# Two transformer blocks on one core: the seams between stages, in what order they issue loads, weight splits and projections

## The chip, the cores and the metric
The kernel runs on one core of a Trainium2 chip. The metric is the device time of one execution in microseconds (us); lower is better. A core has TensorE (PE, matrix products into PSUM banks), VectorE (DVE), ScalarE (ACT), GpSimd (POOL) and SyncE (SP, which only issues transfers). Each engine works off its own list of instructions in order and waits on semaphores of the others.

## The reference, cut to what matters
Two blocks follow each other on 256 tokens of width 1024. The first block has two layers of attention and a mixture of 32 experts, over 256 latent and 256 context tokens; its last layer returns the latent tokens alone. The second block has two layers ("last layers" below) of a mixer with three branches and a gated feed-forward net, each closed by a layer norm.

```python
# first block, end of each layer
h_lat = layer_norm(ALPHA * h_lat + mods[:, :, 5] * y_lat, ln_g[i, 1], ln_b[i, 1])   # y: the experts' output, mods[5]: gate
# second block
for l in range(2):
    mix = hybrid_mixer(x, w_in[l], ...)          # projections a_q, a_k, a_v, ..., attention, conv, MoBA, gates
    x = layer_norm_2(ALPHA_2 * x + mix, ln1_g[l], ln1_b[l])
    ffn = (silu(x @ w_gate) * (x @ w_up)) @ w_down
    x = layer_norm_2(ALPHA_2 * x + ffn, ln2_g[l], ln2_b[l])
```

## The kernel before
Tokens lie in tiles of 128: two latent tiles (`hlat`) and, in the first block, two context tiles (`hctx`). Every dense product is made in three: the activations and the weights are each split into a high part (rounded to fp32r) and a low part (the rest), and `mm3` (lines 178 to 180) adds high x high, high x low, low x high. `project` does this for one weight of 512 (or 256) columns: for each token tile 8 x 3 = 24 products into one bank, then an evacuation.

`dense` (line 166 and 167) fetches one weight in pieces of 1 MB: SP issues the load into a ring of six raw tiles (`wraw`; line 143), ACT copies each half of a piece to its high part (L166), DVE (or POOL where told) subtracts to get the low part (L167). The parts go to tiles `whl` of a pool with six buffers; a weight of 512 columns takes four, the key/value weight of the mixer (`proj{l}` number 13, 256 columns) two. `prefetch` issues loads ahead of their `dense`.

`to_hilo` makes the input of a projection: PE transposes a token tile to two banks (L225), one bank is scaled and shifted by DVE (L235) and one by ACT (L233) with the norm's gain and bias as columns, ACT copies the high part (L238), DVE subtracts for the low part (L239). `normalize` is two DVE statistics (L338), an aggregate (L331), a scale (L211), a power on POOL (L213), and one operation over the tile, on DVE (L341) or on ACT (L345 after L344).

Four places lie around the change.
1. After the first expert stage, `combine` loads for each of four tiles two expert outputs (`y`, L1211) and, once for each pair of tiles, a gate row broadcast to all partitions (L1213), all on SP, with weight loads between (`ahead`). The function that it returns combines one tile (L1219 to L1222) and normalizes it. `layer1_attention` calls it for four tiles; the first weight, `cd_in` 0, is split from the second tile on, and its instructions are put behind the norm of that tile by `issue_after`.
2. After the second expert stage the same `combine` runs for two tiles. `block2(0)` opens its pools (`hi2`, `xT2`, `ev2`), `take` does both tiles, and `mixer2` then projects: weight 13 for both tiles, weight 0 (queries `aq`) for both tiles, weight 1 (`cq`), and so on; attention work fills in between.
3. At the end of layer 0's `ffn2` the four results are added to `hlat` (L1573) and normalized; `block2(1)` opens new pools over the memory of the old ones.
4. At the end of layer 1's `ffn2` each tile is normalized, multiplied by a gain row and shifted by a bias row (L349, L350) and stored from ACT's queue (L1577).

The order of each engine's list is not the order of the calls: a planner (`schedule_with_timeline_sim`) simulates the program, and at each point gives an engine the earliest-called instruction that is ready by its own costs. Loads, splits, transposes and products of neighbouring stages are therefore mixed. A tile pool's buffer is given out again when all users of the old content are done; a new pool over old memory waits in the same way. Expert branches are units that nothing crosses.

## Time and profile before

| | us |
|---|---|
| median of 3 runs (lowest to highest) | 2293.49 (2291.16 to 2294.03) |
| profiled execution | 2294.27 |
| span of its profile | 2292.1 |
| PE busy | 1927.0 (84%) |
| DVE busy | 1005.3 (44%) |
| ACT busy | 732.4 (32%) |
| POOL busy | 263.3 (11%) |

The span is the time from the first to the last instruction of the profiled execution. PE's busy time is that of its products, which overlap a little; its granted clock over the span is 0.919 of full speed on average (full speed or half, the half in pauses and shortly after them). The expert stages, where loads bind, end near 780 and 1302 us; the second block runs from there to the end, with its layers meeting at 1800 us.

### The profile page before, as it was taken

How to read it: one execution, taken by the hardware profiler on the slowest of the kernel's cores; microseconds unless marked ns; L12 is line 12 of the kernel's file. 1: busy time of each engine (PE TensorE's matmuls, PEld its weight loads, DVE VectorE, ACT ScalarE, POOL GpSimd, SP SyncE). 2: the span in 40 equal slices, each digit the busy share in tenths (PEclk: the TensorE clock that was granted, in tenths of full speed). 3: DMA queues.
4: the chain of work that ended last, by engine and by line, in shares of the span. 5: the costliest groups of instructions: out<-in, count | busy, mean ns of one | idle time of the engine just before them, and what ended most of it. 6: DMA issues, size and time to landing. Idle time of an engine off the chain costs nothing. (4 is left out here: it accounts for less than half of the span.)

```text
span 2292.1 us, 27169 instructions
## 1 busy us (share of the span) xinstructions
PE 1927.0 (84%) x10066; PEld 1342.1 (59%) x10066; DVE 1005.3 (44%) x1968; ACT 732.4 (32%) x1304; POOL 263.3 (11%) x205
## 2 busy tenths in 40 slices
PE   6999797777886489976876469998999799998997
PEld 2656476333443267753333157787788677776886
DVE  3346665410000174561000057656554467566554
ACT  2233432100111254410101055544444355434442
POOL 0002401101101152120111002000100020002000
PEclk9999698799998799977998779999999999998999
DMA  9973204454779651157589654354455444354550
GB/s 395 364 298 128 103 28 173 179 196 186 306 287 364 254 228 63 42 203 282 220 341 407 244 218 165 111 183 161 157 184 181 149 158 139 135 176 159 184 179 29
DMA packets 74302, 456.05 MB, mean 199 GB/s; under 512 B 12696, under 2 KB 13244, under 8 KB 23648
## 3 DMA queue, kind: packets, MB, share of 16 engines
q1 hardware_dynamic: 61632, 430.99, 50.0%
q0 software_dynamic: 8816, 14.79, 1.8%
q10 hardware_dynamic: 3632, 7.37, 0.9%
q8 instruction: 132, 2.16, 0.4%
q14 instruction: 90, 0.74, 0.1%
HBM read 452.77 MB, written 13.30 MB: 203 GB/s over the span
## 5 line engine op out<-in xcount | busy, mean ns | idle before, releaser
L167 DVE TENSOR_TENSOR whl<-w,whl 128x1024 fp32r<-128x1024 f32 x312 | 395.5, 1282 | 230.3 <-ACT whl L166 220.2
L166 ACT ACTIVATE whl<-w 128x1024 fp32r<-128x1024 f32 x332 | 344.4, 1057 | 259.9 <-PE bankA L180 208.1
L178 PE MATMUL bankA<-whl,x2h 128*128 128x512 f32 (+1 forms) x864 | 344.2, 399 | 9.7 <-ACT x2h L238 7.3
L180 PE MATMUL bankA<-whl,x2l 128*128 128x512 f32 (+1 forms) x864 | 343.8, 398 | 6.2 <-DVE x2l L239 6.2
L179 PE MATMUL bankA<-whl,x2h 128*128 128x512 f32 (+1 forms) x864 | 340.8, 395 | 0.0
L1073 PE MATMUL bankA<-w,xt 128*128 128x512 f32 x320 | 156.7, 652 | 46.7 <-issue 37.1
L178 PEld LDWEIGHTS bankA<-whl,x2h 128*128 128x128 f32 x864 | 167.7, 194 | 43.7 <-ACT x2h L238 8.3
L180 PEld LDWEIGHTS bankA<-whl,x2l 128*128 128x128 f32 x864 | 166.4, 193 | 40.7 <-DVE x2l L239 7.4
L179 PEld LDWEIGHTS bankA<-whl,x2h 128*128 128x128 f32 x864 | 167.2, 194 | 34.6 <-issue 2.0
L1073 PEld LDWEIGHTS bankA<-w,xt 128*128 128x128 f32 x320 | 66.4, 211 | 134.6 <-issue 133.7
L178 PE MATMUL bankA<-whl,xh 128*128 128x512 f32 (+1 forms) x336 | 132.7, 395 | 5.4 <-ACT xh L238 5.4
L179 PE MATMUL bankA<-whl,xh 128*128 128x512 f32 (+1 forms) x336 | 129.2, 384 | 5.1 <-DVE whl L167 5.1
L180 PE MATMUL bankA<-whl,xl 128*128 128x512 f32 (+1 forms) x336 | 128.2, 385 | 0.1
L1020 PE MATMUL bankA<-w,xt 128*32 128x256 f32 x1216 | 86.4, 428 | 48.8 <-issue 25.4
L414 ACT ACTIVATE p<-bankS,sm 128x256 f32<-128x256 f32 (+2 forms) x160 | 85.7, 537 | 117.7 <-DVE sm L405 60.3
L213 POOL TENSOR_TENSOR sm<-sm,mhalf 128x1 f32<-128x1 f32 (+3 forms) x32 | 32.1, 1004 | 691.4 <-DVE sm L211 679.6
L1020 PEld LDWEIGHTS bankA<-w,xt 128*32 128x32 f32 x1216 | 46.9, 122 | 88.6 <-issue 55.1
L1077 DVE TENSOR_TENSOR s<-s,bankA 128x512 f32<-128x512 f32 x10 | 6.9, 688 | 209.3 <-PE bankA L1073 196.6
L1002 POOL DMA_INDIRECT ybuf<-ys,stab x34 | 34.8, 1023 | 514.8 <-ACT xt L999 126.1
L178 PEld LDWEIGHTS bankA<-whl,xh 128*128 128x128 f32 x336 | 64.5, 192 | 33.0 <-ACT xh L238 7.4
L1024 DVE TENSOR_TENSOR s<-s,bankA 64x256 f32<-64x256 f32 x19 | 8.0, 423 | 169.6 <-ACT s L1023 169.6
L1088 PE MATMUL bankA<-w,ht 128*128 128x512 f32 x160 | 71.3, 599 | 7.8 <-DVE ht L1082 7.8
(462 smaller groups left out, 2921.6 us busy)
## 6 DMA issues: line engine op xcount, KB each, us to landing
w<-in_wmoe SPq DMA_DIRECT2D x174, 1024.0 KB, 15.0
w<-in_wd SPq DMA_DIRECT2D x166, 1024.0 KB, 5.5
w<-in_wmod SPq DMA_DIRECT2D x48, 1024.0 KB, 8.5
y<-ybuf SPq DMA_DIRECT2D x12, 512.0 KB, 10.1
w<-in_rows SPq DMA_DIRECT2D x5, 1024.0 KB, 5.4
w<-mrow SPq DMA_DIRECT2D x7, 512.0 KB, 11.0
fbuf<-w SPq DMA_DIRECT2D x4, 512.0 KB, 2.8
nb<-in_nabias POOLq DMA_DIRECT2D x16, 128.0 KB, 2.4
```

The lines of the kernel that those rows point to most:

```text
L166: nc.scalar.activation(h, s, AF.Copy)
L167: self.low = (eng or nc.vector).tensor_tensor(lo, s, h, ALU.subtract).ins
L178: mm(out, lhsT=xh, rhs=wh, start=start, stop=False)
L179: mm(out, lhsT=xh, rhs=wl, start=False, stop=False)
L180: mm(out, lhsT=xl, rhs=wh, start=False, stop=stop)
L213: self.power = self.nc.gpsimd.tensor_tensor(r, t, self.mhalf[:, :n], ALU.pow).ins
L414: nc.scalar.activation(p[:, :n], s[i][:, :n], AF.Exp, bias=nm[:, i:i + 1], accum_out=ss[:, i:i + 1])
L1002: nc.gpsimd.indirect_dma_start(out=ybuf.rearrange("r (m d) -> (r m) d", m=1 << parts), out_offset=bass.IndirectOffsetOnAxis(ap=stabs[parts ...
L1020: nc.tensor.matmul(acc[r:r + 32], lhsT=xT[:, k, 0:32], rhs=wslice(W, m, k, 256 * f, 256), start=k == 0, stop=k == KT - 1)
L1024: nc.vector.tensor_tensor(s, s, acc[64:128], ALU.mult)
L1073: nc.tensor.matmul(acc[m], lhsT=xT[:, k], rhs=wslice(W, m, k), start=k == 0, stop=k == KT - 1)
L1088: nc.tensor.matmul(yb[m], lhsT=hT[:, k], rhs=w2slice(W, k, m * 512, 512), start=k == 0, stop=k == 3)
```

## The change
- `combine` issues the gate rows first, on ACT's queue, and no longer on SP behind the first `y`; the lists `ahead` are laid out anew: after the first expert stage both pieces of `cd_in` 0 stand behind the first tile's `y`, after the second all first weights stand behind both tiles' `y`.
- `cd_in` 0 is split from the first tile on, behind the norm of that tile.
- `block2` of both layers shares its pools (`second_stage`). At the end of layer 0's feed-forward net, ahead of its norm, layer 1's first two weights (13 and 0) are called (`self.ready`), into the shared six `whl` buffers.
- `mixer2` does `take`, weight 13 and weight 0 for one token tile, then for the other. The pools of the attention buffers, the load of `dists` and the memset of `uT` come after that.
- The last norm is two operations on each half tile: (h - mean) * gain, then that * r + bias, and each half is stored by itself, one from SP's and one from ACT's queue.

```diff
         nc = self.nc
         gates = [tp.tile([P, D], F32, name=f"gate{r}", bufs=1) for r in range(nt // 2)]
         ys = [[tp.tile([P, D], F32, tag=f"y{a}", name="y") for a in range(2)] for tt in range(nt)]
+        for r in range(nt // 2):
+            nc.scalar.dma_start(gates[r], self.mrow[l][r:r + 1, 3].partition_broadcast(P))
         for tt in range(nt):
             for a in range(2):
                 r0 = (a * nt + tt) * P
                 last = nc.sync.dma_start(ys[tt][a], ybuf[r0:r0 + P]).ins
-            if tt % 2 == 0:
-                nc.sync.dma_start(gates[tt // 2], self.mrow[l][tt // 2:tt // 2 + 1, 3].partition_broadcast(P))
             self.prefetch(ahead[tt])
         self.wafter = last
 
...
             xls = [xl, xp.tile([P, KT, 256], F32R, name="xlc")]
             for tt in range(4):
                 last = self.combined(tt)
-                if tt == 1:
+                if tt == 0:
                     with tc.issue_after(last):
                         w0 = self.dense("cd_in", 0, hp)
                 self.to_hilo(self.h(tt), KT, xhs[tt // 2], xls[tt // 2], 0, tt % 2 * P,
...
         return route
 
 
-    def take(self, i, xh, xl, ev):
-        for tt in range(2):
-            if i == 6:
-                self.combined(tt)
-            self.to_hilo(self.hlat[:, tt], KT, xh, xl, 0, tt * P,
-                         cols=(self.lncols[:, i], self.lncols[:, i + 1]), pool=ev)
-        self.after.close()
+    def take(self, i, xh, xl, ev, tt):
+        if i == 6:
+            self.combined(tt)
+        self.to_hilo(self.hlat[:, tt], KT, xh, xl, 0, tt * P,
+                     cols=(self.lncols[:, i], self.lncols[:, i + 1]), pool=ev)
+        if tt == 1:
+            self.after.close()
 
     def residual_rows(self, i):
 
...
         for tt in range(2):
             self.gain_bias(self.hlat[:, tt], rows[:, 0:D], rows[:, D:2 * D], self.nc.gpsimd)
 
-    def block2(self, l):
+    def second_stage(self):
+        tc = self.tc
+        with ExitStack() as ctx:
+            hp, xp, ev = (ctx.enter_context(tc.tile_pool(name=n, bufs=b)) for n, b in (("hi2", 6), ("xT2", 1), ("ev2", 3)))
+            self.ready = None
+            for l in range(2):
+                self.block2(l, hp, xp, ev)
+
+    def block2(self, l, hp, xp, ev):
         tc, nc, io = self.tc, self.nc, self.io
         with ExitStack() as ctx:
-            pool = lambda **k: ctx.enter_context(tc.tile_pool(**k))
-            hp = pool(name=f"hi2{l}", bufs=6)
-            xp = pool(name=f"xT2{l}", bufs=1)
-            ev = pool(name=f"ev2{l}", bufs=3)
-
             def xT():
                 return [xp.tile([P, KT, 256], F32R, tag=f"x{a}", name=f"x2{a}") for a in "hl"]
 
...
             with ExitStack() as c1:
                 self.banks(c1, **BANKS2)
                 self.lane = 1
-                self.take(6 + 4 * l, xh, xl, ev)
                 self.mixer2(l, c1, hp, xh, xl, ev, xT)
             with ExitStack() as c2:
                 self.banks(c2, A=4, B=4)
...
         cw = yp.tile([P, 4, 3], F32, name="cw")
         nc.scalar.dma_start(cw, io["convw"][l])
         with ExitStack() as c1:
-            qp = c1.enter_context(tc.tile_pool(name=f"qk2{l}", bufs=1))
-            pp = c1.enter_context(tc.tile_pool(name=f"pp2{l}", bufs=4))
-            aq = qp.tile([P, 4, 256], F32, name="aq")
-            ak = qp.tile([P, 256], F32, name="ak")
-            cq = qp.tile([P, 4, 256], F32, name="cq")
-            ck = qp.tile([P, 4, 256], F32, name="ck")
-            V = qp.tile([P, 2, 640], F32, name="V2")
-            uT = qp.tile([P, 4, 258], F32, name="uT")
-            bT = qp.tile([P, 4, 256], F32, name="bT")
-            dists = qp.tile([P, 512], F32, name="dists")
-            nc.scalar.dma_start(dists, io["masks"][0])
-            nc.gpsimd.memset(uT[:, :, 0:2], 0.0)
+            qa = c1.enter_context(tc.tile_pool(name=f"qa2{l}", bufs=1))
+            aq = qa.tile([P, 4, 256], F32, name="aq")
+            ak = qa.tile([P, 256], F32, name="ak")
+            V = qa.tile([P, 2, 640], F32, name="V2")
 
             def t_evac(dst, scale):
                 def f(tt, acc):
...
                 nc.vector.tensor_copy(t, acc[:, 0:128])
                 self.transpose_out(t, 1, ak[:, tt * P:tt * P + P].unsqueeze(1))
 
+            tts = range(2)
+            w = self.ready
+            for tt in tts:
+                self.take(6 + 4 * l, xh, xl, ev, tt)
+                if not w:
+                    w = [self.dense(name, 13, hp), self.dense(name, 0, hp)]
+                self.project(w[0], xh, xl, [tt], 256, kva_evac)
+                self.project(w[1], xh, xl, [tt], 512, t_evac(aq, 0.125))
+            qp = c1.enter_context(tc.tile_pool(name=f"qk2{l}", bufs=1))
+            pp = c1.enter_context(tc.tile_pool(name=f"pp2{l}", bufs=4))
+            cq = qp.tile([P, 4, 256], F32, name="cq")
+            ck = qp.tile([P, 4, 256], F32, name="ck")
+            uT = qp.tile([P, 4, 258], F32, name="uT")
+            bT = qp.tile([P, 4, 256], F32, name="bT")
+            dists = qp.tile([P, 512], F32, name="dists")
+            nc.scalar.dma_start(dists, io["masks"][0])
+            nc.gpsimd.memset(uT[:, :, 0:2], 0.0)
+
             def v_evac(tt, acc):
                 nc.scalar.activation(V[:, tt, 0:512], acc, AF.Copy)
 
...
                 nc.vector.tensor_tensor(bh[tt], bh[tt], acc, ALU.mult)
                 self.transpose_out(bh[tt], 4, uT[:, :, 2 + tt * P:2 + tt * P + P])
 
-            tts = range(2)
-            self.project(self.dense(name, 13, hp), xh, xl, tts, 256, kva_evac)
-            self.project(self.dense(name, 0, hp), xh, xl, tts, 512, t_evac(aq, 0.125))
             self.project(self.dense(name, 1, hp), xh, xl, tts, 512, t_evac(cq, 0.125))
             self.project(self.dense(name, 2, hp), xh, xl, tts, 512, t_evac(ck, None))
             self.project(self.dense(name, 3, hp), xh, xl, tts, 512, v_evac)
...
         tc, nc, io = self.tc, self.nc, self.io
         fp = ctx.enter_context(tc.tile_pool(name=f"ffn{l}", bufs=1))
         xh, xl = xT()
-        self.take(8 + 4 * l, xh, xl, ev)
+        for tt in range(2):
+            self.take(8 + 4 * l, xh, xl, ev, tt)
         self.residual_rows(8 + 4 * l)
         gh = fp.tile([P, 22, 256], F32R, name="gh")
         gl = fp.tile([P, 22, 256], F32R, name="gl")
...
                         k = 4 * i + kk
                         wh, wl = sl(kk * D + half * 512, 512)
                         self.mm3(acc[tt][half], gh[:, k, s], gl[:, k, s], wh, wl, k == 0, k == 21)
+        if l == 0:
+            self.ready = [self.dense("proj1", i, hp) for i in (13, 0)]
         for tt in range(2):
             h = self.hlat[:, tt]
-            for half in range(2):
-                hs = h[:, half * 512:half * 512 + 512]
+            halves = [h[:, half * 512:half * 512 + 512] for half in range(2)]
+            for half, hs in enumerate(halves):
                 nc.vector.scalar_tensor_tensor(hs, hs, ALPHA, acc[tt][half], ALU.mult, ALU.add)
-            self.normalize(h)
-            if l == 1:
-                self.gain_bias(h, *rows, nc.vector)
-                nc.scalar.dma_start(io["out"][tt * P:tt * P + P], h)
+            if l == 0:
+                self.normalize(h)
+                continue
+
+            st = self.small.tile([P, 2, 6], F32, tag="bnst", name="bnst", bufs=4)
+            for half, hs in enumerate(halves):
+                nc.vector.bn_stats(st[:, half], hs)
+            mv, r = self.moments(st)
+            for half, hs in enumerate(halves):
+                nc.vector.scalar_tensor_tensor(hs, hs, mv[:, 0:1], rows[0][:, half * 512:half * 512 + 512],
+                                               ALU.subtract, ALU.mult)
+            for half, hs in enumerate(halves):
+                nc.vector.scalar_tensor_tensor(hs, hs, r, rows[1][:, half * 512:half * 512 + 512], ALU.mult, ALU.add)
+                (nc.scalar if half else nc.sync).dma_start(
+                    io["out"][tt * P:tt * P + P, half * 512:half * 512 + 512], hs)
 
 
     def moe_scope(self, l, nt):
...
                 self.experts(l, nt, ep, W, meta, meta2, gtab, stabs, XG, XE, ybuf)
             self.wextra = None
             cw.close()
-        ahead = ([[("cd_in", 0, 0)], [("cd_in", 0, 1), ("cd_in", 1, 0), ("cd_in", 1, 1)], [], []] if l == 0 else
-                 [[("proj0", 13, 0)], [("proj0", 0, 0), ("proj0", 0, 1)]])
+        ahead = ([[("cd_in", 0, 0), ("cd_in", 0, 1)], [("cd_in", 1, 0), ("cd_in", 1, 1)], [], []] if l == 0 else
+                 [[], [("proj0", 13, 0), ("proj0", 0, 0), ("proj0", 0, 1)]])
         tp = self.after.enter_context(tc.tile_pool(name=f"ct{l}", bufs=2, side="right"))
         self.combined = self.combine(l, ybuf, rw, nt, ahead, tp)
 
...
             self.banks(ctx, **BANKS1)
             self.layer1_attention(ctx, lambda: self.streams.pop().__exit__(None, None, None))
         self.moe_scope(1, 2)
-        for l in range(2):
-            self.block2(l)
+        self.second_stage()
         self.streams.pop().__exit__(None, None, None)
```

## Rows read from the trace of the kernel before

**Rows 1.** Stretches: window, length, busy (count) by engine, PE clock, DMA, GB/s.
```profile
785.00:812.00 27.00, 4.59 (x13) 3.34 (x14) 16.98 (x22) 13.92 (x17) 9.22 (x5) 0.50 0.95 377
...
812.00:848.00 36.00, 33.04 (x157) 25.80 (x156) 27.64 (x37) 18.16 (x31) 23.40 (x15) 0.98 0.52 206
...
1302.00:1340.00 38.00, 3.21 (x14) 2.81 (x15) 18.97 (x28) 12.99 (x16) 5.49 (x5) 0.54 0.83 330
...
1363.00:1588.00 225.00, 217.33 (x1033) 174.08 (x1032) 143.00 (x275) 108.11 (x195) 12.42 (x4) 0.98 0.45 154
...
1800.00:1813.00 13.00, 3.38 (x19) 2.83 (x18) 12.48 (x20) 8.21 (x12) 4.39 (x3) 0.75 0.52 177
...
1836.00:2065.00 229.00, 221.25 (x1039) 176.94 (x1040) 144.86 (x276) 109.44 (x196) 15.63 (x8) 0.98 0.44 152
```

**Rows 2.** Timeline, 1304 to 1364: start, us, engine, line, operation, tiles, [idle <-releaser].
```profile
1304.91 0.35 ACTq L1402 DMA_DIRECT2D cw<-in_convw  x1
...
1309.08 1.40 SPq L1213 DMA_DIRECT2D gate<-mrow  x1
...
1316.82 1.23 DVE L1221 TENSOR_TENSOR y<-y,gate 128x1024 f32<-128x1024 f32 x1 [2.09 <-DMA gate<-mrow]
...
1319.43 2.00 ACT L166 ACTIVATE whl<-w 128x1024 fp32r<-128x1024 f32 x2 [6.10 <-DMA w<-in_wd]
...
1331.56 0.68 DVE L239 TENSOR_TENSOR x2l<-a,x2h 128x512 fp32r<-128x512 f32 x1
...
1335.62 0.68 DVE L239 TENSOR_TENSOR x2l<-a,x2h 128x512 fp32r<-128x512 f32 x1
...
1338.76 1.97 PE L225 MATMUL bankA<-cst,hlat 128*128 128x128 f32 x8 [11.07 <-ACT hlat L345]
...
1340.38 0.56 PE L178 MATMUL bankA<-whl,x2h 128*128 128x256 f32 x1
...
1342.88 1.29 DVE L239 TENSOR_TENSOR x2l<-a,x2h 128x512 fp32r<-128x512 f32 x2 [1.60 <-ACT x2h L238]
...
1363.16 0.47 PE L178 MATMUL bankA<-whl,x2h 128*128 128x512 f32 x1
```

**Rows 3.** Timeline, 1796 to 1813.
```profile
1796.30 0.69 DVE L1573 SCALAR_TENSOR_TENSOR hlat<-hlat,bankA 128x512 f32<-128x512 f32 x1 [8.55 <-PE bankA L180]
...
1801.30 5.79 ACT L166 ACTIVATE whl<-w 128x1024 fp32r<-128x1024 f32 x6 [15.37 <-DVE hlat L1573]
...
1802.18 1.06 PE L225 MATMUL bankA<-cst,hlat 128*128 128x128 f32 x8 [1.84 <-DVE hlat L341]
...
1806.23 3.48 DVE L167 TENSOR_TENSOR whl<-w,whl 128x1024 fp32r<-128x1024 f32 x3
...
1806.39 3.73 POOL L213 TENSOR_TENSOR sm<-sm,mhalf 128x1 f32<-128x1 f32 x1 [5.20 <-DVE sm L211]
...
1807.00 1.48 ACT L233 ACTIVATE a<-bankA,lncols 128x128 f32<-128x128 f32 x4
...
1811.03 1.97 PE L225 MATMUL bankA<-cst,hlat 128*128 128x128 f32 x8 [7.78 <-DVE hlat L341]
...
1812.65 0.56 PE L178 MATMUL bankA<-whl,x2h 128*128 128x256 f32 x1
```

**Rows 4.** Timeline of PE, 793 to 844.
```profile
810.17 0.79 PE L179 MATMUL bankA<-whl,xh 128*128 128x512 f32 x1 [4.67 <-DVE whl L167]
...
843.45 0.77 PE L225 MATMUL bankB<-cst,hctx 128*128 128x128 f32 x5 [0.95 <-ACT hctx L345]
```

**Rows 5.** Timeline of DVE at the end; last line: the stores' time to landing.
```profile
2279.10 1.21 DVE L349 TENSOR_TENSOR hlat<-hlat,fln 128x1024 f32<-128x1024 f32 x1
...
2282.29 0.81 DVE L341 TENSOR_SCALAR hlat<-hlat,sm 128x1024 f32<-128x1024 f32 x1 [0.66 <-POOL sm L213]
...
2284.40 1.23 DVE L350 TENSOR_TENSOR hlat<-hlat,fln 128x1024 f32<-128x1024 f32 x1
...
DMA to landing us min/median/max: 2.6/2.6/2.6
```
## The prediction

> **What bounds the kernel now.** I began with the page's slices: TensorE (PE) is busy 84% of the span, and the slices where it is not are the two expert stages and the seams between stages. So I cut the span with the view of stretches [rows 1]. Inside the two mixers of the second block PE works 217.33 of 225 us and 221.25 of 229 us; there nothing but PE's own work counts. At the seams it hardly works: 4.59 of 27 us after the first expert stage, 3.21 of 38 us after the second, 3.38 of 13 us between the two last layers. The change touches these three seams and the very end, so I read the timeline of each: what PE waits for, and what the instruction that it waits for stood behind. The chain that ended last names little outside the last seam, so I do not lean on it.
>
> Each seam has one shape. Token tile 0 is combined or normalized (DVE), transposed (PE), scaled and split in a high and a low part (ACT, DVE); tile 1 follows; the first weights are split by the same ACT and DVE; only then do the products start. The order in every engine's list is fixed ahead, so an instruction that is ready can stand behind one that is not.
>
> **Seam 2, experts to the second block** [rows 2]. Three edits meet here.
> First the order on PE. The products of tile 0 begin at 1340.38, right behind the transposes of tile 1, for which PE idled 11.07 us. But tile 0 was ready long before: its two low halves ended at 1331.56 + 0.68 = 1332.24 and 1335.62 + 0.68 = 1336.30. With projections by token tile, PE meets tile 0's products before tile 1's transposes. The four groups (key/value and query weights, each for two tiles, 24 products each) run from 1340.38 to the third weight's first product at 1363.16: 22.78 us, 11.39 per tile, of which a third (3.8) is the key/value group with its 256 columns. That group can start at 1332.3 but not enter its second half before 1336.3, so it starts in effect at 1336.3 - 1.9 = 1334.4; tile 0 is through at 1345.8. Tile 1 is ready at 1342.88 + 1.29 = 1344.17 and so does not delay it; tile 1 is through at 1357.2. That is 6.0 us earlier than 1363.16.
> Second the gate. DVE waits 2.09 us for the gate row, which SP issues at 1309.08 behind two y transfers. ACT issues a small load at 1304.91, 4.2 us sooner, and has no other work till the y tiles are there. Nothing stands behind the gate on ACT's queue but that load and the scaling of y, which waits for y anyway. If the gate's tile is free when ACT comes to it, all 2.09 us go; if ACT must wait for the experts' last scatter as SP does, the gate runs beside y and the 0.5 MB that it takes (1.4 us at the 377 GB/s of rows 1) comes off y's pace: 0.7 us are left. I take 2.1, since ACT's list shows the earlier issue; bounds 0 and 2.1.
> The Trainium skill, "DMA: Bandwidth & Descriptors", section "Issuing engines are not separate DMA queues", speaks against this edit: queues of several engines run on the same 16 DMA engines and interleave, so another queue saves only issue time. The trace of before has no gate on ACT's queue and cannot show it; by that rule the sum below would be 18.6 in place of 20.0.
> Third, what lies between tile 0's two low halves: 1335.62 - 1332.24 = 3.4 us of DVE, splits of weights and tile 1's statistics. In the changed program the first splits come after tile 0 and the y tiles of tile 1 are issued before any weight. This can take the 3.4 us away or leave them: half, 1.7.
> Against it: the two first weights fill all six split buffers (two and four), and the third weight's first split must now wait for the key/value group of tile 1, one group later than before. It needs two ACT copies (2.00 for two) and a DVE subtraction (1.2, a third of the 3.48 of rows 3), and has the query group of tile 1, 7.6 us, as cover: nothing, or 2.0 if that cover is full.
> Seam 2: 6.0 + 2.1 + 1.7 = 9.8; bounds 4.0 (order alone, less 2.0) and 13 (the 3.4 us whole and a further 1.5 from tile 1's work lying under tile 0's products).
>
> **Seam 3, layer 0 to layer 1** [rows 3]. Now the six ACT copies of the first weights wait 15.37 us and run only at 1801.30 to 1807.09, after the last products' results are read, because the new layer's buffers open there. Tile 0's transposes end at 1802.18 + 1.06 = 1803.24, and its ACT scaling stands behind these copies until 1807.00. Three subtractions (3.48) run at 1806.23, and beside them POOL's power for tile 1 takes 3.73 us, so tile 1 is transposed at 1811.03 and PE starts at 1812.65. With shared buffers and the splits called ahead of the norm, four of six copies and subtractions (4 x 1.2 = 4.9) run under the last matmuls, in DVE's idle 8.55 us; the last two need buffers that the last matmuls still read and run right after them. From 1803.24 tile 0 needs its scaling (1.5), a copy and a subtraction (0.6 and 0.7 as in rows 2): 1805.8 at best; the two remaining subtractions (2.4) in front of it give 1808. I take 1806.6, 6.0 us before 1812.65. Tile 1 then has 11.4 us of cover, more than its norm and split need. Seam 3: 6.0; bounds 4.6 and 6.8.
>
> **Seam 1, experts to the first block's second layer** [rows 4]. PE's first product is followed by 4.67 us of waiting, until 810.17, for a low part of the weights, because those subtractions are called behind the norm of tile 1. Behind the norm of tile 0 they come about 8 us sooner and the 4.67 us go. But DVE does the same work in all: 27.64 of 36 us busy, and POOL 23.40, in the stretch after [rows 1], and PE's next wait of note, 0.95 us at 843.45, is for the last context tile, at the end of that DVE list. The subtractions (4.9 us) now stand in front of tile 1's work; and 1 MB of weights goes ahead of tile 1's y, 2.8 us at 377 GB/s. I take about half, 2.5; bounds -2.8 (only the delay) and 4.7. The gates on ACT's queue I cost at nothing here: they now leave at the same time as y.
>
> **The end** [rows 5]. Norm, gain and bias are 0.81 + 1.21 + 1.23 = 3.25 us per tile. The new form is four half-tile operations; the nearest row is the 0.69 us of the same operation at 512 columns [rows 3]: 2.76, 0.5 less, 1.0 for both tiles. The 0.66 us that DVE waits for the power can be filled by the operation that needs only the mean, unless POOL is held up beside it as at 1806.39: 0 to 0.66, I take 0. The last store is half as long: 256 KB less at 377 GB/s, 0.7 of the 2.6 us. End: 1.7; bounds 1.0 and 2.4.
>
> The later loads and the memset of the attention buffers move behind the first projections, whose 22.78 us hide them; if late they would hold the first scores, not the projections.
>
> **Sum.** 9.8 + 6.0 + 2.5 + 1.7 = 20.0 us. The profiled run took 2294.27 us (span 2292.1): 2274.3. It lies 0.8 above the median of the runs shown, so 2273.5 for a median. The low ends together give 6.8 us, the high ends 26.9.
>
> **Rivals.**
> A: tile 1 becomes what PE waits for. Splits and tile 1's work fill DVE at both late seams, and only the order's bare part is left: 4.0 at seam 2, 4.6 at seam 3; with 2.5 and 1.7, 12.8 us: 2280.7. For it: DVE works 12.48 of 13 us at seam 3. Against: six of its subtractions, at 3.48 / 3 each, are the splits, and four of them move away.
> B: the transfers bind. Weights ahead of y cost 2.8 at seam 1, and the gates beside y leave 0.7 of 2.1 at seam 2: 20.0 - 5.3 - 1.4 = 13.3, 2280.2. For it: DMA is 95% busy at seam 1. Against: at seam 2 ACT can issue first. The skill's page on DMA named above says the same of the gates.
> C: the change does not do what it says, since the fixed lists again put both tiles' transposes first. Then 2.1 at seam 2, the 3.8 us of ACT's scaling at seam 3, nothing at seam 1, 1.7: 7.6, 2285.9. Against: tile 1's call now stands behind tile 0's products.
> D, the other side: slower. Both mixers' lists, where attention fills in between projections, are laid out anew, and fit worse. PE idles 7.7 and 7.75 us there; at 90% busy it would idle 22.5 and 22.9, which costs 30 us against the sum: 2303.5. It decides from 24.6 us lost (20.0 and the 4.6 of a measurable change). Against: the two mixers begin behind seams of 38 and 13 us and idle the same to 0.1 us [rows 1].
> E: more than the sum: all high ends, 26.9: 2266.6.
>
> **Numbers.** Forecast 0.57, A 0.18, B 0.09, C 0.06, D 0.05, E 0.05. The range reaches past A and B on one side and to E on the other, a little further for what rows cannot price: 2264 to 2285. A measurement tells 0.2% (4.6 us) from no change. Faster: all but D and half of C: 0.91; same: half of C less a little: 0.03; slower: D and what I do not see: 0.06.
>
> **What would show it.** Right: after the second expert stage PE's first product near 1329, tile 0's query products before tile 1's transposes, no DVE wait for a gate; at seam 3 four weight copies before the last matmul ends and first product 4 to 7 us after tile 0's transposes began; mixers of 225 and 229 us as before. Wrong: idle gaps of PE in front of tile 1's products as long as the old ones, a gap at the third weight's first product, a first-layer stage no shorter by its last context tile, or mixers with more than 8 us idle.

## The result, and the profile after

The changed kernel is slower: 2306.07 us (median of 5 runs, 2303.94 to 2307.23) against 2294.03 for the kernel before beside it (2291.16 to 2296.34); ratio 1.0053, 95% interval 1.0039 to 1.0066. The forecast was 2273.5. The span of the profiled execution went from 2292.1 to 2305.4 us, PE's busy time from 1927.0 to 1932.0.

Where the 13.3 us of span arose is seen by matching the products of the two traces and taking how much later each starts after the change: -1.3 us ahead of the first expert stage's end, +15.6 from 860 to 1300, +15.1 at 1510, +14.9 at 1790, +12.5 at 1990, +13.0 at the last matmul. So seam 1 lost 16.9, seam 2 gained 0.5, seam 3 gained 2.4, and the end nothing; the stretches between moved by 0.5 us at most. The stretches of [rows 1], moved by about these shifts, with the mixers again from the third weight's first product (columns as there):

```profile
784.00:811.00 27.00, 7.68 (x21) 5.59 (x22) 15.53 (x20) 12.79 (x16) 5.62 (x3) 0.50 0.97 373
811.00:864.00 53.00, 36.31 (x152) 29.12 (x151) 37.01 (x40) 19.59 (x33) 29.56 (x17) 0.80 0.44 162
1318.00:1356.00 38.00, 7.44 (x34) 6.55 (x34) 19.05 (x28) 13.72 (x17) 6.23 (x5) 0.55 0.83 332
1381.00:1604.00 223.00, 216.19 (x1027) 174.57 (x1027) 140.95 (x253) 105.99 (x185) 12.38 (x4) 0.98 0.46 158
1813.00:1826.00 13.00, 4.17 (x18) 3.07 (x16) 11.02 (x20) 3.71 (x7) 1.54 (x3) 0.72 0.71 256
1858.00:2078.00 220.00, 213.21 (x1028) 172.89 (x1028) 140.68 (x253) 105.99 (x185) 16.02 (x8) 0.99 0.47 158
```

The mixers idle 6.8 us each (7.7 before): they are not what became slower. The second row is: 53 us in place of 36, of which PE idles 16.7 (3.0 before) and works 36.3 (33.0 before). Its granted clock is at half of full speed (1.2 in place of 2.4 GHz) until 811.7, and again, with the waits below, from 818.6 to 828.8 and from 852.7 to 862.9; before, it rose at 813.3 and stayed up.

**Seam 1**, PE's timeline, then DVE's, then POOL's [rows 4 for before]:

```profile
806.51 0.80 PE L180 MATMUL bankA<-whl,xl 128*128 128x512 f32 x1 [0.91 <-DVE xl L239]
...
820.10 1.97 PE L225 MATMUL bankB<-cst,hlat 128*128 128x128 f32 x8 [5.87 <-ACT hlat L345]
824.24 0.79 PE L178 MATMUL bankA<-whl,xh 128*128 128x512 f32 x1 [2.17 <-ACT xh L238]
...
858.27 1.97 PE L225 MATMUL bankB<-cst,hctx 128*128 128x128 f32 x8 [8.24 <-ACT hctx L345]
```
```profile
804.57 1.28 DVE L1220 SCALAR_TENSOR_TENSOR y<-y,rw 128x1024 f32<-128x1024 f32 x1
...
809.32 3.39 DVE L1222 SCALAR_TENSOR_TENSOR hlat<-hlat,y 128x1024 f32<-128x1024 f32 x1 [2.26 <-POOL y L1221]
...
816.48 2.29 DVE L344 SCALAR_TENSOR_TENSOR sm<-sm 128x1 f32<-128x1 f32 x1 [0.45 <-POOL sm L213]
...
847.72 9.23 DVE L344 SCALAR_TENSOR_TENSOR sm<-sm 128x1 f32<-128x1 f32 x1 [1.54 <-POOL sm L213]
```
```profile
805.99 3.30 POOL L1221 TENSOR_TENSOR y<-y,gate 128x1024 f32<-128x1024 f32 x1 [7.96 <-DVE y L1220]
809.25 5.70 POOL L167 TENSOR_TENSOR whl<-w,whl 128x1024 fp32r<-128x1024 f32 x2
...
847.63 4.71 POOL L349 TENSOR_TENSOR hlat<-hlat,w 128x1024 f32<-128x1024 f32 x2
852.28 4.63 POOL L350 TENSOR_TENSOR hlat<-hlat,w 128x1024 f32<-128x1024 f32 x2
```

And the last tile's L344 in the trace of before:

```profile
839.75 2.37 DVE L344 SCALAR_TENSOR_TENSOR sm<-sm 128x1 f32<-128x1 f32 x1 [0.69 <-POOL sm L213]
```

The wait of 4.67 us for the low part is gone, as forecast. In its place PE waits 5.87 and 2.17 us for tile 1 and 8.24 for the last context tile. Tile 1's L1220 runs at 804.57 (before 798.86), behind four splits. Of these 5.7 us, 3.6 are its late y, which landed at 801.01 (before 798.23) and was scaled by ACT until 802.43 (before 798.82); 2.1 are the splits. From there it needs 14.2 us to the end of its L344 where before it needed 10.1: L1222, 1.2 us by itself, lasts 3.39 beside POOL's splits, while L338, which reads one tile and not two, keeps its 1.28 us for two halves beside them. The last tile's L344, an operation on 128x1 elements that takes 0.16 us by itself, lasts 9.23 us: it ends at 856.95, when the last of POOL's four row operations ends (856.91). In the trace of before it lasted 2.37, until the first of the four ended.

**Seam 2** [rows 2 for before; add 15.6 to those times], PE and DVE:

```profile
1343.56 1.97 PE L225 MATMUL bankA<-cst,hlat 128*128 128x128 f32 x8 [26.80 <-ACT hlat L345]
1348.90 0.58 PE L178 MATMUL bankA<-whl,x2h 128*128 128x256 f32 x1 [3.36 <-ACT x2h L238]
...
1350.63 0.58 PE L180 MATMUL bankA<-whl,x2l 128*128 128x256 f32 x1 [0.94 <-DVE x2l L239]
...
1362.88 1.04 PE L225 MATMUL bankA<-cst,hlat 128*128 128x128 f32 x8
...
1366.09 0.38 PE L178 MATMUL bankA<-whl,x2h 128*128 128x256 f32 x1 [1.75 <-ACT x2h L238]
...
1368.38 0.79 PE L395 MATMUL bankS<-ak,aq 64*128 64x128 f32 x2 [1.79 <-ACT p L414]
```
```profile
1331.33 1.28 DVE L1220 SCALAR_TENSOR_TENSOR y<-y,rw 128x1024 f32<-128x1024 f32 x1 [18.27 <-DMA y<-ybuf]
1332.65 1.22 DVE L1221 TENSOR_TENSOR y<-y,gate 128x1024 f32<-128x1024 f32 x1
```

Tile 0's products do run ahead of tile 1, 7 us sooner than before. But tile 1's transposes (1362.88) stand in PE's list behind tile 0's query products, though the tile was ready at 1352.45, so its scaling and splitting begin only then and PE waits 1.75 us for its high part. The next wait, 1.79 us, is of another kind: a score product of the attention that fills in waits for ACT's p, and p stands in ACT's list behind the scaling of tile 1 and a table load of 1.28 us. The granted clock, at full speed from 1354.5, is at half again from 1368.1 to 1374.9, behind these two waits. The third weight's first product comes at 1383.00, by the shift of 15.6 us 4.2 later than before and not sooner; some of the attention's products now stand ahead of it (1027 products are left in the mixer's stretch, before 1033), and that stretch is 2 us shorter.

**Seam 3** [rows 3], DVE and PE:

```profile
1817.01 1.22 DVE L167 TENSOR_TENSOR whl<-w,whl 128x1024 fp32r<-128x1024 f32 x1
...
1818.75 1.21 DVE L167 TENSOR_TENSOR whl<-w,whl 128x1024 fp32r<-128x1024 f32 x1
1819.87 0.20 DVE L331 BATCH_NORM_AGGREGATE sm<-bnst 128x2 f32<-128x12 f32 x1
```
```profile
1822.31 1.94 PE L225 MATMUL bankA<-cst,hlat 128*128 128x128 f32 x8 [7.08 <-DVE hlat L341]
1826.37 0.58 PE L178 MATMUL bankA<-whl,x2h 128*128 128x256 f32 x1 [2.11 <-ACT x2h L238]
...
1842.98 0.38 PE L178 MATMUL bankA<-whl,x2h 128*128 128x256 f32 x1 [1.69 <-ACT x2h L238]
1845.27 0.48 PE L395 MATMUL bankS<-ak,aq 64*128 64x128 f32 x2 [1.79 <-ACT p L414]
```

The splits run early, but the last two of them and the additions of tile 1 stand in front of tile 0's norm (L331). The two waits of seam 2 are here again, 1.69 and 1.79. PE starts 1.2 us sooner than before (1826.37 less the shift of 14.9 is 1811.5, against 1812.65).

**The end** [rows 5]: DVE is done 1.6 us sooner against the last matmul, and the last store lands 2.1 sooner. The span does not end sooner: in POOL's queue the closing drain begins with its last power and lasts 10.02 us (9.58 before), and the span ends 1.0 us behind it (0.9 before).

```profile
2294.45 0.99 POOL L213 TENSOR_TENSOR sm<-sm,mhalf 128x1 f32<-128x1 f32 x1 [3.29 <-DVE sm L211]
```

### The profile page after: what moved, and what is told of

It reads as the page before. It is cut to its first block, busy times and chain, and to the rows that moved or that the text cites. A ratio compares the mean times of both kernels' runs of the same rounds, so it can differ in the third digit from the quotient of the medians.

```text
span 2305.4 us, 27190 instructions
## 1 busy us (share of the span) xinstructions
PE 1932.0 (84%) x10066; PEld 1347.2 (58%) x10066; DVE 1009.4 (44%) x1970; ACT 731.8 (32%) x1304; POOL 263.8 (11%) x205
## 5 line engine op out<-in xcount | busy, mean ns | idle before, releaser
L178 PE MATMUL bankA<-whl,x2h 128*128 128x512 f32 (+1 forms) x864 | 345.6, 401 | 18.6 <-ACT x2h L238 16.3
```

The source lines that it names most:

```text
L178: mm(out, lhsT=xh, rhs=wh, start=start, stop=False)
```

## The experiments

Theory from the trace of the changed kernel: seam 1 lost 17 us because the early split moved operations of DVE and POOL that read two tiles from SBUF, the on-chip memory, beside each other; rivals: the transfers (weights ahead of y, gates on ACT), or the later stages. Each ratio is against the kernel before on the same chip in the same session; "us" is the ratio less one, times 2293. "Seam 1" is the loss there by matched products in the one profiled execution of each kernel, against the one of before.

| kernel | median us | us against before [95%] | seam 1 |
|---|---|---|---|
| the changed kernel | 2306.07 | +12.2 [+8.9, +15.1] | +16.9 |
| seam1_as_before | 2290.40 | -2.8 [-6.0, +0.5] | 0 |
| split_early_alone | 2305.20 | +12.2 [+8.3, +16.1] | +14.7 |
| loads_early_alone | 2300.87 | +6.6 [+3.4, +9.9] | +8.5 |
| weights_ahead_alone | 2310.27 | +17.0 [+14.0, +20.2] | +16.8 |
| rows_after_scale | 2298.13 | +6.9 [+4.1, +9.4] | +11.4 |
| gate1_on_dve | 2291.77 | -0.5 [-3.2, +2.5] | +7.6 |
| no_pool_seam1 | 2296.08 | +1.4 [-1.4, +4.4] | +5.9 |
| dve_only_seam1 | 2295.80 | +4.1 [+0.9, +7.3] | +4.2 |
| no_pool_before | 2297.07 | +4.6 [+1.8, +7.1] | +6.7 |
| last_norm_alone | 2292.11 | -0.9 [-3.4, +1.4] | -0.7 |
| last_norm_off_pool | 2286.69 | -5.5 [-8.7, -2.3] | +8.5 |
| take_before_queries | 2285.38 | -7.6 [-10.3, -4.8] | -0.3 |
| splits_behind_norm | 2289.83 | -3.9 [-6.2, -1.4] | -0.5 |
| late_end_rows | 2292.05 | -1.1 [-3.4, +0.9] | +6.7 |
| end_rows | 2294.88 | +1.6 [-0.5, +3.9] | +8.4 |
| no_pool_all | 2289.74 | -3.9 [-6.6, -1.4] | +5.2 |
| no_pool_end | 2293.71 | -0.9 [-3.2, +1.1] | +4.7 |
| dve_only_all | 2288.50 | -4.4 [-7.3, -1.4] | +3.2 |

**Which part of seam 1.** Undone in the changed kernel, or done alone in the kernel before:

```diff
 seam1_as_before (on after): gates of l == 0 on SP, ahead of l == 0 and "if tt == 1" as before
 split_early_alone (on before):
-                if tt == 1:
+                if tt == 0:
 weights_ahead_alone (on before; loads_early_alone has the gates of l == 0 on ACT's queue too):
-        ahead = ([[("cd_in", 0, 0)], [("cd_in", 0, 1), ("cd_in", 1, 0), ...
+        ahead = ([[("cd_in", 0, 0), ("cd_in", 0, 1)], [("cd_in", 1, 0), ...
```


> The changed kernel with the seam after the first expert stage put back to that of before: gates on SP behind y, both pieces of cd_in 0 around tile 1's y, its split from the second tile on. The late seams and the end stay changed. Theory (the loss is all in that seam: matched products of PE stand 15.7 us late behind it and 1.3 early ahead of it): 2306.1 - 17.0 = 2289, some 5 us below the kernel before, and the last context tile is transposed at the old time. Rival (the loss lies in the later stages, and what the seam loses would have been lost there anyway): within 4 us of 2306.

> The kernel before with one line changed: cd_in 0 is split from the first tile on. Loads and gates as before. Theory of the order (the four splits in front of tile 1's combination, and POOL's operations beside DVE's, cost the 17 us): 2294 + 10 to 17 = 2304 to 2311. Rival of the transfers (the cost is in loads ahead of y and gates on ACT): 2289 to 2295, since the 4.67 us wait for the low part goes.

> The kernel before with the first seam's transfers alone changed: gates on ACT's queue ahead of y, and the second piece of cd_in 0 ahead of tile 1's y. The split stays where it was. Theory of the order: 2294, up to 3 more for tile 1's y (2.8 us late in the trace of after). Rival of the transfers: 2304 to 2311.

> The kernel before with the second piece of cd_in 0 issued ahead of tile 1's y, gates on SP as before. loads_early_alone, with the gates on ACT as well, was 8 us above before. If the weights ahead of y are the cost: 5 to 8 above. If the gates beside y are: within 2 of before.

The loss lies in seam 1: seam1_as_before wins back 15.0 us timed and all of the 16.9 in the profile. But each of its two parts, done alone, loses as much or more, the split 12.2 and the weights ahead of y 17.0, so neither theory stands alone, and the two losses are not shares of one sum: each kernel also waits where the changed one does not. With the split alone PE waits 7.14 us for tile 0's low half, which stands behind splits and tile 1; with the weights ahead alone it waits 12.12 for the low part of the weights (4.67 before), still called behind a tile 1 that is now later:

```profile
813.59 0.80 PE L180 MATMUL bankA<-whl,xl 128*128 128x512 f32 x1 [7.14 <-DVE xl L239]
820.97 0.80 PE L179 MATMUL bankA<-whl,xh 128*128 128x512 f32 x1 [12.12 <-DVE whl L167]
```

What the two have in common is in DVE's rows: with the split alone L344 of the last tile lasts 9.19 us, with the weights ahead alone 9.17 (DVE's rows of split_early_alone):

```profile
847.17 9.19 DVE L344 SCALAR_TENSOR_TENSOR sm<-sm 128x1 f32<-128x1 f32 x1 [1.81 <-POOL sm L213]
```

In loads_early_alone, with the gates on ACT as well, the same row lasts 2.33 and the loss is less than half as large. The gates on ACT are thus not the cost.

**The long row.** The four row operations are called behind the small scale (`last`) and no longer behind POOL's power; then also tile 1's gate product goes to DVE.

```diff
-            with tc.issue_after(self.power):
+            with tc.issue_after(last):
                 self.residual_rows(2)
 gate1_on_dve adds:
-            (nc.gpsimd if tt else nc.vector).tensor_tensor(y[0], y[0], gates[tt // 2], ALU.mult)
+            (nc.gpsimd if tt > 1 else nc.vector).tensor_tensor(y[0], y[0], gates[tt // 2], ALU.mult)
```


> The changed kernel with one line changed: POOL's four gain and bias operations on the latent tiles (L349, L350, 2.3 us each) are called behind DVE's small operation of the last context tile (L344), and no longer behind the power alone. Theory (in the trace of after this 128x1 operation is held for 9.23 us beside those four, and PE waits 8.24 us for what follows): the wait shrinks to below 1 us, 7.5 us less than the changed kernel, so about 6 us above the kernel before in place of 13. Rival (the tile is late for its own reasons, the long row only fills a wait): no change, 12 to 14 us above.

> rows_after_scale (the changed kernel with the four row operations behind the last scale), and tile 1's gate product (L1221) on DVE in place of POOL. Theory (half of tile 1's delay of 9.8 us at the first seam is DVE and POOL holding each other up: from L1220 to the end of L344 it takes 14.2 us in after, 10.1 before): 3 to 4 less than rows_after_scale, 3 above before. Rival (the delay is the place in DVE's list alone, so more work on DVE only makes it later): as rows_after_scale, 7 above, or more.

POOL's and DVE's rows of rows_after_scale:

```profile
826.47 4.76 POOL L349 TENSOR_TENSOR hlat<-hlat,w 128x1024 f32<-128x1024 f32 x2
...
836.91 3.40 POOL L350 TENSOR_TENSOR hlat<-hlat,w 128x1024 f32<-128x1024 f32 x1
...
851.40 0.16 DVE L344 SCALAR_TENSOR_TENSOR sm<-sm 128x1 f32<-128x1 f32 x1 [1.53 <-POOL sm L213]
```

The times came near the theory, the second well below it: L344 of the last tile is back to 0.16 us and PE's wait of 8.24 to 1.17. But the edit did not do what its words say. `last` is an instruction of DVE and the rows are POOL's; taken from behind the power, they run 11 us and more ahead of the last L344, not behind it. L344 is free because the rows have left its side, and they hold the third tile's L344 instead (2.33 us) while the last one comes 3.7 us later than in the changed kernel. The same holds for every kernel below with this edit. In gate1_on_dve, with one POOL operation less, tile 1's L344 starts at 814.56 in place of 816.48 and is not held.

**POOL out of the seam.** First gate products and cd_in 1 on DVE, and the four row operations by the edit above; in no_pool_seam1 POOL runs these from 817.38, where they hold the third tile's L344 for 2.29 us and two low halves of tile 1 for 4.79 (1.28 by themselves). So a second pair puts these on DVE too.

```diff
-            (nc.gpsimd if tt else nc.vector).tensor_tensor(y[0], y[0], gates[tt // 2], ALU.mult)
+            (nc.gpsimd if l and tt else nc.vector).tensor_tensor(y[0], y[0], gates[tt // 2], ALU.mult)
-            w1 = self.dense("cd_in", 1, hp, nc.gpsimd)
+            w1 = self.dense("cd_in", 1, hp)
 dve_only: residual_rows(2) on nc.vector; no_pool: called behind the last small scale as above
```


> The changed kernel with POOL's two-operand work taken out of the first seam: gate products (L1221) of the first stage and the low parts of cd_in 1 on DVE, the four row operations behind the last small scale. Theory (the loss of 17 us is DVE and POOL holding each other up, set off by the early split; without POOL, tile 1's scale comes near 811 in place of 818.8 and the last context tile near 840 in place of 857): 14 to 20 less than the changed kernel, 2 to 8 below before. Rival (the splits' place and the late y are the cause): DVE has 8.6 us more work, so no better than gate1_on_dve, at or above before.

> The kernel before with the same three edits of the first seam. Theory (its wait of 4.67 us holds 2.1 us of L344 beside POOL, and its next waits a part each): 3 to 4 below before, and a narrower spread of its runs than before, whose spread of 13 us comes from which engine gets ahead there. Rival (POOL takes work off a full DVE): above before by 2 to 6.

> The changed kernel with no two-operand work of POOL left in the first seam: gate products and low parts of cd_in 1 on DVE as in no_pool_seam1, and the four row operations on DVE too (in no_pool_seam1 they had only moved forward in the seam, and held L344 for 2.3 and two splits for 2.9 us). Theory (each engine holds the other up): no DVE row of the seam lasts longer than alone (1.2 us, 0.7, 0.16), and 4 to 8 less than no_pool_seam1, which was 2 above before: 2 to 6 below before. Rival (order and late y; DVE now has 13.5 us more work than in after): no gain on no_pool_seam1 or a loss, 2 to 8 above before.

DVE's rows of dve_only_seam1, and the stretches of its seam 1:

```profile
804.49 1.28 DVE L1220 SCALAR_TENSOR_TENSOR y<-y,rw 128x1024 f32<-128x1024 f32 x1
...
810.29 1.22 DVE L1222 SCALAR_TENSOR_TENSOR hlat<-hlat,y 128x1024 f32<-128x1024 f32 x1
...
816.99 0.16 DVE L344 SCALAR_TENSOR_TENSOR sm<-sm 128x1 f32<-128x1 f32 x1 [0.45 <-POOL sm L213]
...
842.18 0.16 DVE L344 SCALAR_TENSOR_TENSOR sm<-sm 128x1 f32<-128x1 f32 x1 [1.91 <-POOL sm L213]
```
```profile
785.00:811.00 26.00, 7.77 (x21) 5.68 (x22) 17.88 (x23) 12.79 (x16) 0.60 (x1) 0.50 0.99 386
811.00:852.00 41.00, 34.92 (x156) 27.98 (x155) 29.45 (x48) 20.69 (x35) 5.01 (x7) 0.90 0.56 208
```

No row is held: L1222 is back to 1.22, L344 to 0.16, and with all of POOL's row work DVE is busy for 47.3 us (17.88 + 29.45) of the seam, where it was busy for 52.5 (15.53 + 37.01) in the changed kernel. Seam 1 costs 4.2 us in place of 16.9: 12.7 went with DVE and POOL holding each other up, in one execution of each kernel. What is left is the order and the late y, as the rival had it: tile 1's L344 is still at 816.99, since the four splits, two more and the context tile's operations stand in front of it. The timed gain is smaller, 8.1 us from +12.2 to +4.1, with intervals of 3 us each side; the forecast of a time below before failed. gate1_on_dve, which moves less off POOL, won back 12.7 timed and 9.3 in its profile, so the size of the hold-up is known to some 4 us only. no_pool_before lost 4.6 us, in the range of its rival, but the rival's reason (POOL takes work off a full DVE) is not shown: its four rows run early too, and in end_rows below that edit alone costs seam 1 8.4 us.

**The end.**

```diff
 last_norm_alone (on before): the last norm's part of the change
 last_norm_off_pool adds:
-            mv, r = self.moments(st)
+            mv, r = self.sm(2), self.sm(1)
+            nc.vector.bn_aggr(mv, st)
+            nc.vector.tensor_scalar(r, mv[:, 1:2], 1.0, LN_EPS, ALU.mult, ALU.add)
+            nc.scalar.activation(r, r, AF.Sqrt)
+            nc.vector.reciprocal(r, r)
```


> The kernel before with the last norm in two operations per half tile, stores by halves, and nothing else. By the prediction's term for the end: 2294.0 - 1.7 = 2292.3. By the theory formed from the trace of after, where the span ends 10.0 us after POOL's drain began and the drain begins with the last power: the power comes no sooner, so 2294.0 within 0.7, though the last store lands about 1.6 us earlier.

> The kernel with the last norm alone changed, and its power (POOL) replaced by a square root on ACT and a reciprocal on DVE, so that POOL has nothing to do at the end. Theory (the span ends with POOL's drain, 10.0 us from the last power, while all other engines are through 4.9 us sooner): 4 to 5 us less than last_norm_alone, about 2287.5. Rival (the drain is as long behind whatever comes last, or the end is set by the stores): 2292 within 1.

From the first addition of the last norm to the end of the span it takes 19.25 us before (2272.85 to 2292.1), 19.57 in the changed kernel, 19.51 in last_norm_alone and 14.76 without POOL; the five other kernels with that end have 14.8 to 15.0. In last_norm_off_pool, no row of POOL stands at the end, and the span ends 3.3 us behind the issue of the last store:

```profile
2285.60 1.41 DVE L1592 SCALAR_TENSOR_TENSOR hlat<-hlat,sm,fln 128x512 f32<-128x512 f32 x2
2287.10 0.35 ACTq L1593 DMA_DIRECT2D out<-hlat  x1
```

The theory of the drain is shown by the spans, and the timed results agree: 4.6 us between last_norm_alone and last_norm_off_pool, with intervals of 2 to 3 us each side.

**The late seams.** Both on seam1_as_before.

```diff
 take_before_queries: take(0), w[0] of tile 0, take(1), w[1] of tile 0, w[0] and w[1] of tile 1
 splits_behind_norm: self.ready = [...] moved behind the loop over tt
```


> The changed kernel with the first seam as before (seam1_as_before), and at both late seams tile 1 is taken (combined, transposed, split) between tile 0's key/value products and tile 0's query products. Theory (tile 1, long ready, is transposed only behind the query products, PE then idles 3.5 us at each seam and falls to half its clock): 7 to 12 us less than seam1_as_before, 2278 to 2283. Rival (what the seam gains is given back in the mixer, since attention work used as filling is used up early in either case): 2287 to 2291.

> seam1_as_before with the first two weights of layer 1 called behind the norms of both tiles, not ahead of them. Theory (in the trace of after, splits stand ahead of tile 0's norm on DVE and delay its scale by 5.3 us): splits still run in DVE's idle time under the last products, the norm comes 5 us sooner and so do the products: 2285 to 2286. Rival (the splits are needed as soon as the norm, so the wait only changes its name): 2289 to 2292.

Between products that match (one at 1298, one at 1510; one at 1790, one at 1990) the stretches of before, of the changed kernel and of take_before_queries are:

```profile
1298.00:1510.00 212.00, 170.25 (x851) 134.11 (x848) 126.02 (x255) 100.87 (x193) 17.90 (x9) 0.91 0.45 162
1790.00:1990.00 200.00, 184.15 (x895) 146.81 (x894) 125.18 (x255) 96.54 (x190) 16.78 (x7) 0.96 0.40 137
```
```profile
1313.60:1525.10 211.50, 173.00 (x851) 137.79 (x848) 125.49 (x255) 100.56 (x193) 18.87 (x9) 0.90 0.46 163
1804.90:2002.50 197.60, 181.09 (x896) 146.10 (x895) 124.09 (x255) 95.92 (x190) 13.93 (x7) 0.96 0.41 138
```
```profile
1300.70:1511.10 210.40, 171.42 (x851) 135.61 (x848) 126.27 (x255) 100.17 (x193) 18.89 (x9) 0.91 0.46 164
1789.20:1988.80 199.60, 182.01 (x895) 145.90 (x894) 125.38 (x255) 95.51 (x190) 13.93 (x7) 0.96 0.40 137
```

In the changed kernel PE idles 3.3 us less in the first stretch (38.5 against 41.75) but is 2.75 busier with the same 851 products: more of them run at half the clock. Taking tile 1 earlier removes both waits and the second fall of the clock, and in that trace the products of the seam run some 5 us sooner against seam1_as_before; by 1450 it is given back, 3.2 us of it in a wait of 1.94 us for DVE at 1413.97 and one of 1.25 for ACT at 1440.39. Against before the profiles give it 2.0 us in the two seams together, the changed kernel 2.9 and seam1_as_before 3.9, so by the profiles it is a loss of 1.9; the timed runs give it 4.8 us more than seam1_as_before, measured in another session. Whether it is worth anything stays open. In splits_behind_norm the planner wrote the same list of DVE, with the splits in front of L331 again, so it says nothing on their price.

**Parts together.**

> First seam as before but for POOL's four row operations behind the last small scale; both late seams changed, with tile 1 taken ahead of tile 0's queries; the last norm without POOL. If the parts add by their medians (take_before_queries 7.5 below the kernel before, 4.6 for POOL's drain, 1 for the rows): 13 below before. If the late seams are worth only what their profiles show between the first and the last matched product of each (1 to 3 together): 7 to 9 below.

> The kernel before with the last norm in half tiles without POOL, and POOL's four row operations behind the last small scale; no late seam changed. 5.5 + 1 = 6.5 below before. Beside late_end_rows it tells what the late seams' new order is worth: 6 us if the medians add, 1 to 3 if the mixers give back what the seams gain.

> The whole change, with the three edits of the first seam, tile 1 taken ahead of tile 0's queries, and the last norm without POOL. If the parts add: no_pool_seam1 less 4.6 for POOL's drain, less 0 to 3 for the late seams: 7 to 15 below before. If the mixers give back the late seams: as no_pool_seam1 less 4.6.

> The kernel before with the three edits of the first seam and the last norm in half tiles without POOL, no late seam changed: no_pool_before less 4.6, 7 to 9 below before. Beside no_pool_all it tells what the rest of the change (early split, loads, late seams) is worth.

> As dve_only_seam1, with tile 1 taken ahead of tile 0's queries at the late seams and the last norm without POOL. 4.6 for the drain and 0 to 3 for the late seams less than dve_only_seam1; no_pool_all was 4 below before. By the theory 8 to 13 below before, by the rival within 4 of before.

The parts do not add. late_end_rows, expected 7 to 13 below before, and end_rows, expected 6.5 below, came out level with it: in both the row operations now stand early in seam 1, which costs 6.7 and 8.4 us there in the profiles. no_pool_end, expected 7 to 9 below, is level too. dve_only_all, the whole change cleared of what went wrong, is faster than before (-4.4, its interval clear of zero) and so than the changed kernel, but short of the 8 to 13 expected; the rest of the change is worth 3 us in the pair no_pool_all and no_pool_end, whose intervals of 2 to 3 us each side overlap. last_norm_off_pool, the last norm alone, gains as much.

## Why the prediction was wrong

1. **Seam 1, +2.5 forecast, -16.9.** The step that failed is the lower bound. The working had that the subtractions would "stand in front of tile 1's work" and charged their 4.9 us and 2.8 for the weights; it did not ask which POOL operations they would then run beside. The trace of before had the price: rows of L344 of 2.3 us, a power of 3.73 [rows 3], POOL busy 23.40 of 36 us [rows 1]. What the runs showed in its place is the hold-up of DVE and POOL: without POOL's row work seam 1 costs 4.2 us, order and late y, near the bound of -2.8, and the other 12.7 (8.1 timed) are gone.
2. **Seam 2, order, 6.0.** Tile 0 was through at 1361.70; forecast 1345.8 + 15.6 = 1361.4. That is right for the order alone, but the gate and the gap, 3.8 together, should have brought it sooner and did not. "Tile 1 is ready ... and so does not delay it" failed: it was ready, but its transposes stood behind the query products, so PE waits 1.75 us for its high part and 1.79 for ACT's p behind it. The sum also took every product at full clock.
3. **Gate, 2.1, and gap, 1.7.** The wait for the gate is gone, and nothing is gained (L1221 runs at 1332.65, before 1316.82 + 15.6 = 1332.42): y lands 5.36 and 6.93 us after its issue (3.87 and 4.70 before), and ACT's gate did not leave ahead of y: it left at 1323.90, 0.03 us behind the first y, after the experts' last scatter as SP's loads do. The rule weighed there, of the Trainium skill, "DMA: Bandwidth & Descriptors", section "Issuing engines are not separate DMA queues", has that queues of several engines interleave on the same 16 DMA engines. The trace agrees, since y landed later beside the gate. By it the sum would have been 18.6. The gap between tile 0's two low halves did close, but five splits now stand ahead of tile 0's scaling (two before): L344 runs 1.8 us after its power's end (at once before) and L235 3.3 us after the transposes begin (1.2 before), 3.9 us together, as much as both terms.
4. **Seam 3, 6.0, gained 2.4.** The four early splits came as forecast. The two that were to stand in front of tile 0's scaling stood in front of its norm, with tile 1's additions, and tile 1 again stood behind the query products.
5. **End, 1.7, gained 0.** The operations took 0.74 for 0.69 and the stores came sooner, as said; the term was counted to DVE's last row and the last landing, and the span hangs on POOL's drain, which begins with the last power.
6. **Rivals.** B was right that the gates of seam 2 gain nothing and that y comes later at seam 1 (2.8 us at tile 1); the weights ahead cost more than its 2.8 when done alone, and not by the transfer alone, but by DVE's list and POOL's rows. D ended at 2303.5, close to the measured time, but by a mechanism that did not occur: the mixers idle no more than before. The slower case that came true was not among the rivals.

## What to carry to other kernels

Before an operation is moved to an earlier place, look at which operations of the other engine will run beside it there (here of DVE and POOL): a small operation in front of a tile was held for as long as the neighbour's whole row of work. When an edit of the order helps, read in the trace where the operations went: four rows that were meant to run behind a scale ran ahead of it. Where the trace shows an engine's order, check for each tile not only that its data are ready but where its transposes stand in PE's list, and count the first products after a pause at half the clock, as in the seams here. At the end of a kernel, follow every engine's queue to its last record, not the last store.

## What was not expected of the hardware

- A DVE operation on 128x1 elements was held 9.17 to 9.32 us beside four POOL operations in a row, but 2.3 us in other traces. What goes with it is POOL's list just before: in the four traces of the long row POOL passes from its DMA issues (L1294) to the power without a gap, in the six of the short row it idles 0.20 to 0.26 us first, and L344 then starts 0.06 us behind the first row operation and not 0.08. Whether that is the cause was not tested. In last_norm_off_pool, whose seam 1 is the code of before, it was held too, and seam 1 cost 8.5 us:

```profile
836.30 9.32 DVE L344 SCALAR_TENSOR_TENSOR sm<-sm 128x1 f32<-128x1 f32 x1 [3.50 <-POOL sm L213]
```

  So part of the spread of the kernel before (2283 to 2301 us over all its runs) can come from this; that was not tested. POOL is held as well: a split of 2.3 us lasted 6.84 in that trace. The Trainium skill, "SBUF — State Buffer", section "SBUF: two separate sides", has that DVE operations with two SBUF inputs and GpSimd operations that read SBUF lock a port pair against each other for a whole instruction. The rows agree (2.3 us of L344 is one POOL operation, and no DVE row of dve_only_seam1 is held), and add that the waiting one can lose to several instructions in a row: the 9.2 to 9.3 us are four.
- POOL's closing drain lasts 9.58 us (before) and 10.02 us (after) from its last small power, and 5 us of it lie behind the last landing of a store (2299.15 in the changed kernel, whose drain ends at 2304.43).
